# Memory keys and values of both layers from operands in two parts, the weights' second part made by a load that adds onto the negative of the first

## The chip, the cores and the metric

The program runs on one core of a Trainium2 chip. Its engines work side by side, each on its own list of instructions in order: TensorE (PE in the profile; its weight loads are PEld), VectorE (DVE), ScalarE (ACT), GpSimd (POOL) and SyncE (SP), which here only issues DMAs. An instruction starts when its engine has reached it and the semaphores that it waits for are there. The metric is the time of one execution on the device in microseconds (us), lower is better; the median of three runs is given with the lowest and the highest.

## The reference

One step of a streaming encoder of two layers, 1024 channels, 512 prompt tokens and 32 sample tokens. Layer 0 mixes tokens by an S5 state-space model with a gated output (GLU), layer 1 by retention. Each layer then attends to 256 memory tokens and ends in a ConvFFN. What the change touches are the memory's keys and values, which depend on the memory tokens and on weights alone:

```python
def memory_kv(mem, g_mem, w_kv):
    b, n, _ = mem.shape
    m = rms_norm(mem, g_mem).astype(F32) @ w_kv.astype(F32)
    k, v = jnp.split(m, 2, axis=-1)
    return k.reshape(b, n, MEM_HEADS, MEM_HD), v.reshape(b, n, MEM_HEADS, MEM_HD)
...
for i in range(DEPTH):
    ...
    xp = xp + yp                      # S5 or retention
    mkp, mvp = memory_kv(mem_prompt, norm_mem_kv[i], mem_w_kv[i])
    xp = xp + memory_attn(rms_norm(xp, norm_mem_q[i]), mkp, mvp, mem_w_q[i], mem_w_o[i])
```

What stands beside it in time is S5: a complex diagonal recurrence in 64 groups of 16 channels with 64 states each, `x[t] = a x[t-1] + b u[t]`, of which the output is the real part of `c x` and a direct term.

## The kernel before

**Products in two parts.** Most matrix products take each float32 operand as two float32r numbers, `hi` and `lo`, with `hi + lo` the operand, and add three products: hi·hi, hi·lo, lo·hi (`mm3`, L224 to L226). `weights` (L209) makes the parts of a weight tile of 128 x 1024: SyncE loads it into a buffer `wr` (L211), ScalarE copies it into `wh` as float32r (L206), and VectorE subtracts, `wl = wr - wh` (L207). There are three buffers each of `wr`, `wh` and `wl` in the whole program, used in turn.

**Phase 1** (`phase1`) holds S5 and, as fill for TensorE between S5's steps, the memory's projections of both layers. `kv_units` gives the latter as units: for each layer the operand (gain times memory, in eight pieces), then eight key tiles and eight value tiles, each with one weight tile of 512 KB. `KV_SPLIT` names the layers that work in two parts. Before it holds layer 1 alone. Layer 0's weights are just loaded, and one float32 product per piece is taken (L500); its operand is gain times memory by ScalarE. Layer 1's weights go through `weights`, its operand is made in two parts (ScalarE, then VectorE at L476), and its products are those of `mm3`. `product` (L495 to L500) chooses. The call `fill(us)` emits units until about so many microseconds of TensorE's work are used up, 3.5 for a tile: 0.5 at the start, 28 behind the discretisation, 2 and 13 around the norm of the inputs, and then what `PROLOGUE` and `ORDER` say.

**S5's steps** work on an eighth of the groups each, e = 0 to 7:

- `matrices(e)`: GpSimd scales the inputs, `u` (L781); VectorE multiplies powers of `a` with `b` (L789, L790), into buffers of the tags `wh` and `wl`, the same three each that the weights use; GpSimd adds (L791); TensorE turns the result (L797) and multiplies it with `c` (L802); ScalarE copies out (L798); GpSimd and VectorE make `Fg` (L807, L809), and eight DMAs lay it out.
- `states(e)`: TensorE multiplies with the inputs (L823); VectorE and GpSimd turn the result by phases (L834 and on for VectorE; L836, L839 and the copies L840, L841 for GpSimd); VectorE scans (L847, twice); both turn it back; GpSimd copies the states out (L859, L860).
- `carry(e)`: VectorE multiplies (L873 and on), GpSimd adds (L877). `outputs(e)`: TensorE multiplies (L888, L889), ScalarE applies gelu and copies.

The powers of phases that `states` needs are made once (`phases`; GpSimd's share stands at L553 and L556). The loop runs e from 0 to 7 in the order `S(e+1), C(e+1), O(e), F 4, M(e+2), F 5`, where F n is `fill(n)`; what is left of the units comes behind it. A scheduler then puts the instructions of the whole program into one order for each engine, by the dependences and the buffers; the order is fixed when the kernel is built.

**Behind phase 1** come GLU and everything else: `dense` products (L233) of the same form, with `weights` for each tile.

Of the kernel before, what the change touches and what calls it, by code (L numbers as in the profile page):

```python
# [9 lines left out]
F32 = mybir.dt.float32  # L10
# [7 lines left out]
P = 128  # L18
D = 1024
KT = D // P            # channel tiles  # L20
TP = 512               # prompt tokens
TS = 32                # sample tokens
# [3 lines left out]
NM = 256               # memory tokens  # L26
FF = 2816
NF = FF // P
H = 4                  # heads (memory attention and retention)
EPS = 1e-6  # L30
GN_EPS = 1e-5
G = 64                 # S5 groups
C = 16                 # channels of a group
NP = 32                # pairs of groups
L = 8                  # S5 chunk
POS = 70               # dummy, 64 prompt chunks, dummy, 4 sample chunks
SLOT = 560             # elements of a general slot
# phase 1: microseconds of TensorE's work on the memory's projections between the steps of S5
F_START, F_DISC, F_NORM, F_MAT = 0.5, 28, 2, 13
KV_US = 3.5  # L40
KV_SPLIT = (1,)          # layers whose memory projections take operands in two parts
KV_RMS, KV_ROW = 1, 4      # key tiles after which the memory's norm is worked out, and applied
# steps of S5 for an eighth of the groups (M matrices, P phases, S states, C carry, O outputs, F fill)
PROLOGUE = (("M", 0), ("P", 0), ("S", 0), ("M", 1), ("C", 0), ("F", 6))
ORDER = (("S", 1), ("C", 1), ("O", 0), ("F", 4), ("M", 2), ("F", 5))
FGROUPS = (8, 7, 7)    # ConvFFN tiles between down projections
# [6 lines left out]
def constants():  # L53
    """Arrays that depend on shapes alone."""
# [27 lines left out]
def w_tiles(w, mt=None):  # L82
    """[K, M] -> [m tile, 128 of k, K/128 * 128 of m]: one contiguous chunk for an output tile."""
    k, m = w.shape
    a = w.reshape(k // P, P, m // P, P).transpose(2, 1, 0, 3)
    return a.reshape(m // P, P, (k // P) * P)


def layout(inp):
# [10 lines left out]
    def cols(a):                      # [.., n*128] -> [128, .. * n]  # L100
        a = a.reshape(-1, a.shape[-1] // P, P)
        return a.transpose(2, 0, 1).reshape(P, -1)
# [3 lines left out]

    def pair(a):                      # [G, 64] -> [(g2, p), pair]
        return a.reshape(NP, P).T

    def both(a):                      # [G, 64] -> [(2, p), G]  # L110
        return np.concatenate([a.T, a.T], axis=0)
# [7 lines left out]
    cr, ci = f["ssm_c_re"][0], f["ssm_c_im"][0]      # [G, C, 64]  # L119
# [6 lines left out]
    rt, it = cr.transpose(2, 0, 1), ci.transpose(2, 0, 1)          # [64, G, C]  # L126
    ca = np.stack([np.concatenate([rt, it]), np.concatenate([it, rt])])   # [2, 128, G, C]
    d["ca"] = ca.reshape(2, P, KT, 8 * C).transpose(2, 1, 0, 3).reshape(KT, P, 256)

    def rows(a):                      # [1024] -> [(jj, c), G]  # L130
        return np.tile(a.reshape(G, C).T, (L, 1))

# [6 lines left out]
    # values: [layer, half of columns, quarter of k, 128, 2 k tiles * 512]  # L139
# [13 lines left out]
    d["w_r"] = w_tiles(wq)            # q 8, k 8, v 16, g 16 tiles  # L153
# [17 lines left out]
class Kernel:  # L171
# [7 lines left out]
    # ---- tiles  # L179
# [13 lines left out]
    def psum(self, name, two, one):  # L193
        """TensorE's accumulators of a part of the program: two banks each, and one each."""
        self.two, self.one = two, one
        return self.tc.tile_pool(name=name, bufs=1, space=PSUM)
# [7 lines left out]
    # ---- weights: loaded, and split into parts of 12 and 12 bits  # L204
# [15 lines left out]

    def mm3(self, out, a, b, start, stop):
        """out (+)= a^T b for operands in two parts."""
# [20 lines left out]
    def dense_open(self, src, xs):  # L243
        """The first operands of an output tile."""
        o = [self.ps(), self.weights(src), 0]
        self.dense_more(o, xs)
        return o
# [7 lines left out]
    def dense2(self, srcs, xs, late=1, hooks=()):  # L255
        """Two output tiles, the last operands of both behind all others; hooks go in between."""
# [15 lines left out]
    def parts(self, src):  # L272
        """src [P, T] -> its two parts, in general slots."""
# [4 lines left out]
    # ---- norms: operands are gain * x; 1 / rms comes in where a product leaves PSUM  # L278
# [29 lines left out]
    def rsqrt_of(self, m, r, tmp):  # L308
        """r = m^-1/2: a first guess from the exponent's bits, and three steps r <- r (1.5 - 0.5 m r^2)."""
# [13 lines left out]
    def resid_cols(self, ps):  # L323
        """1 / rms of the tokens, 128 of them in a column; ps [128, 5] of PSUM."""
# [12 lines left out]
    def along_row(self, ps, rc, blocks):  # L337
        """Columns rc laid along the free dimension of all partitions, in PSUM."""
# [3 lines left out]
    def resid_r(self):  # L342
        """Two hooks that give 1 / rms of the tokens along a row of all partitions, self.r."""
# [19 lines left out]
    # ---- program  # L363
# [28 lines left out]
    def final(self):  # L392
        """The last norm: turned to tokens by rows, scaled by 1 / rms where it leaves PSUM."""
# [30 lines left out]
    # ---- memory keys and values  # L424
    def kv_units(self):
        """The projections of both layers, in pieces that fill gaps: (microseconds of TensorE, emit)."""
# [22 lines left out]
        def rms():  # L449
            """1 / rms of the memory's tokens: along a row, and in columns."""  # L450
# [14 lines left out]
        def operand(l):  # L465
            """gain * memory"""
# [21 lines left out]
        def weights(l, src):  # L488
            if l in KV_SPLIT:
                return self.weights(src)  # L490
# [4 lines left out]
        def product(l, out, a, ca, b, cb, k):  # L495
            """out (+)= a[:, ca]^T b[:, cb], in one or in two parts."""
# [50 lines left out]
    # ---- S5  # L547
    def cmul(self, eng, o, a, b, t, eng2=None):
        """o = a b of complex pairs; t: two temporaries of the same shape. o may not alias a or b."""
# [9 lines left out]
    def phase1(self, sp):  # L559
# [43 lines left out]
        # inputs in the S5 layout: [(7 - token of chunk, channel), group, chunk]  # L603
# [4 lines left out]
        # discretisation, for columns of pairs (32) and of groups (64)  # L608
# [8 lines left out]
        def exp_acc(out, x, t):  # L617
            """exp to float32's accuracy: 2^k times a polynomial."""
# [33 lines left out]
        # powers 0..8 of a = rho (cos, sin)  # L652
# [18 lines left out]
        # b_bar = (a - 1) / lam * b, times the norm's gains  # L671
# [23 lines left out]
        # u = x / rms(x)  # L695
# [26 lines left out]
        # unit phases of a^8 to the power of the chunk, and its magnitude  # L722
# [7 lines left out]
        def unit(c):  # L730
            """c / |c|, for |c| near 1"""
# [43 lines left out]
        def matrices(e):  # L775
            """What a chunk's inputs give to the state at its end, and to its own outputs."""
# [5 lines left out]
            # a^lag b_bar, as [(g2, p), pair, lag, c]; the second holds minus the imaginary part  # L782
# [31 lines left out]
        def states(e):  # L814
            """Chunk inputs to the state, turned back by the chunk's phase, scanned, turned forth."""
# [46 lines left out]
        def carry(e):  # L862
            """What the state before a chunk gives to its tokens: Re(c a^(l+1) x)."""
# [72 lines left out]
    # ---- memory attention  # L936
    def attention(self, ap, l):
# [33 lines left out]
        def soft(rows, b0, b1, src, pr, st):  # L971
            """Softmax of scores / 16, whose queries still lack 1 / rms."""
# [30 lines left out]
        def turn(pr, pss):  # L1003
            """The weights, keys by rows."""
# [4 lines left out]
            # the sample's, from the cache  # L1009
# [53 lines left out]
    # ---- ConvFFN  # L1063
    def ffn(self, l):
# [11 lines left out]
        for n, size in enumerate(FGROUPS):  # L1076
            ys = []
            for _ in range(size):
# [3 lines left out]
                # [2 zeros, prompt, 2 cached rows, sample]  # L1082
# [26 lines left out]
    # ---- retention  # L1109
    def retention(self, rp):  # L1110
# [26 lines left out]
        def rope(tile0):  # L1137
            """Two tiles of a projection, rotated: in float32, and in parts."""
# [32 lines left out]
        def scores(d, h):  # L1171
            d.decay = decay = st([P, TP], "decay")
            nc.sync.dma_start(out=decay, in_=io["decay"][h])
            # keys by token, with the decay to the end
# [14 lines left out]
            # the sample's scores  # L1189
# [4 lines left out]
            # scores with decay, [key, query]  # L1194
# [34 lines left out]
        def outputs(d, h):  # L1229
            """By token, normalised."""  # L1230
# [48 lines left out]
        def gated(d, h):  # L1279
            """By feature."""  # L1280
# [61 lines left out]
def collect(o):  # L1342
    y = o["y"]
    ssm = o["ssm"].reshape(2, 64, 2, G).transpose(2, 0, 3, 1)         # [segment, re/im, G, 64]
# [17 lines left out]
```

## Time and profile before

| | |
|---|---|
| median of 3 runs | 1894.64 us (1894.32 to 1896.23) |
| span of the profiled execution, first to last instruction | 1893.0 us |
| mean granted TensorE clock | 0.980 |
| 0 to 247.86 us (up to the first product of GLU): PE, DVE, ACT, POOL busy | 192.63, 224.00, 74.28, 165.22 us |
| 247.86 to 1893.00 us: PE, DVE, ACT, POOL busy | 1627.52, 862.66, 537.28, 219.50 us |

Of the profiled execution only the span is given, and no time of its own beside it. How to read the profile: a row of a group names the line, the engine, the operation, output and inputs by the program's names, the shape and how often it came; then busy us, the mean of one in ns, and the idle time of the engine ahead of it with what ended it. A row of the timeline begins with the start in us, counted from the first instruction, and the length; in brackets stands what the engine waited for. Rows of stretches have the busy time of each engine, the granted clock and the DMA engines' share. A DMA row ends in the median of the time from issue to landing. Names are without buffer numbers: `wr`, `wh`, `wl` are those of above, `u` the inputs, `xl` the turned matrices, `r` and `xh` general slots.

### The profile page before, as it was taken

Reading aid. Unit: us, or ns where it says so; the run is one execution under the profiler, and the core shown is the slowest. Engines: PE = TensorE matmul, PEld = TensorE weight load, DVE = VectorE, ACT = ScalarE, POOL = GpSimd, SP = SyncE. Lnnn points to the kernel's source line nnn. Section 1 sums busy time; section 2 is a strip of 40 time slices with the busy share of each in tenths; the row PEclk is TensorE's granted clock in tenths of the full one; section 3 lists DMA queues with packets and bytes.
Section 4 is the critical chain, followed back from the end, with each engine's and each line's share of the span. In section 5 each row is a group of like instructions: output and inputs, shape, how many; then the busy total and the mean of one; then the engine's idle time right before and its main releaser. Section 6 shows DMA issues by size and latency. Waiting matters only on the chain.

```text
span 1893.0 us, 32752 instructions
## 1 busy us (share of the span) xinstructions
PE 1820.2 (96%) x13785; PEld 1730.6 (91%) x13785; DVE 1086.7 (57%) x1848; ACT 611.6 (32%) x901; POOL 384.7 (20%) x439
## 2 busy tenths in 40 slices
PE   7868899999999999999999999999999999999998
PEld 6457789999999999999899899998999999999998
DVE  9999856545544535555644646546655554453553
ACT  3132454433323323333223122223444332232333
POOL 7685611011211202121000100100101121120221
PEclk9888989999999999999999999999999999999998
DMA  6434344122222222232222222222411222222221
GB/s 214 132 114 124 120 133 144 68 86 79 90 90 88 78 92 90 72 109 82 76 85 94 79 79 73 90 79 86 138 68 56 87 84 88 90 84 95 90 71 67
DMA packets 65970, 178.02 MB, mean 94 GB/s; under 512 B 8928, under 2 KB 18528, under 8 KB 65824
## 3 DMA queue, kind: packets, MB, share of 16 engines
q1 hardware_dynamic: 65536, 175.79, 27.4%
q8 instruction: 108, 1.77, 0.4%
q14 instruction: 38, 0.31, 0.1%
q10 hardware_dynamic: 288, 0.15, 0.0%
HBM read 162.78 MB, written 10.77 MB: 92 GB/s over the span
## 4 chain that ended last, share of the span: by engine, by line
PE 83%; DVE 2%; issue 1%; ACT 1%; ACTq 0%; DVEq 0%
PE ps L233 74%; PE ps L224 2%; PE ps L225 2%; PE ps L226 2%; PE ps L1286 1%; DVE wl L207 0%; PE ps L1275 0%; PE ps L1248 0%; PE ps L1008 0%; PE ps L1222 0%; ACT wh L206 0%; PE bank L1022 0%; DVE xl L292 0%; PE ps L329 0%; PE ps L403 0%
## 5 line engine op out<-in xcount | busy, mean ns | idle before, releaser
L206 ACT CAST wh<-wr 128x1024 fp32r<-128x1024 f32 (+1 forms) x256 | 264.6, 1037 | 810.2 <-PE ps L233 626.8
L233 PE MATMUL ps<-xh,wh 128*128 128x272 f32 x2432 | 507.5, 290 | 5.4 <-DVE x L356 3.6
L233 PE MATMUL ps<-xl,wh 128*128 128x272 f32 x2432 | 503.6, 288 | 0.0
L233 PE MATMUL ps<-xh,wl 128*128 128x272 f32 x2432 | 502.3, 288 | 0.0
L233 PE MATMUL ps<-r,wh 128*128 128x272 f32 x2688 | 449.2, 289 | 3.0 <-ACT r L901 1.6
L233 PEld LDWEIGHTS ps<-xh,wh 128*128 128x128 f32 x2432 | 380.7, 188 | 11.1 <-ACT r L298 3.7
L233 PEld LDWEIGHTS ps<-r,wh 128*128 128x128 f32 x2688 | 380.2, 189 | 6.4 <-ACT r L206 3.0
L233 PEld LDWEIGHTS ps<-xh,wl 128*128 128x128 f32 x2432 | 382.0, 188 | 2.3 <-issue 2.3
L233 PEld LDWEIGHTS ps<-xl,wh 128*128 128x128 f32 x2432 | 383.0, 189 | 0.3
L207 DVE TENSOR_TENSOR wl<-wr,wh 128x1024 fp32r<-128x1024 f32 (+1 forms) x256 | 321.8, 1260 | 92.3 <-ACT wh L206 84.2
L233 PE MATMUL ps<-r,wl 128*128 128x272 f32 x1344 | 278.0, 288 | 0.0
L233 PEld LDWEIGHTS ps<-r,wl 128*128 128x128 f32 x1344 | 211.2, 189 | 0.0
L356 DVE TENSOR_TENSOR x<-ps,x 128x544 f32<-128x544 f32 x96 | 69.3, 724 | 234.9 <-PE ps L233 234.7
L301 POOL TENSOR_TENSOR acc<-acc,r 128x544 f32<-128x544 f32 x36 | 58.8, 1633 | 453.1 <-ACT r L298 444.6
L1088 POOL COPY nco<-r 128x2 f32<-128x2 f32 x44 | 13.9, 315 | 374.5 <-DVE r L1086 374.5
L1095 DVE TENSOR_TENSOR r<-ps,rr 128x544 f32<-128x544 f32 x44 | 31.9, 725 | 96.7 <-PE ps L233 96.7
L1085 DVE TENSOR_TENSOR r<-ps,rr 128x272 f32<-128x272 f32 x44 | 19.4, 442 | 117.4 <-PE ps L233 117.4
L1146 POOL TENSOR_TENSOR r<-r,r 128x544 f32<-128x544 f32 x8 | 10.8, 1353 | 339.9 <-ACT wh L206 326.0
L1096 POOL TENSOR_TENSOR r<-r,r 128x32 f32<-128x32 f32 x44 | 34.3, 780 | 206.2 <-ACT wh L206 186.2
L206 ACT CAST r<-r 128x544 fp32r<-128x544 f32 x84 | 52.5, 650 | 65.8 <-POOL r L1096 26.2
L1093 DVE SCALAR_TENSOR_TENSOR r<-r,conv,r 128x546 f32<-128x546 f32 x88 | 69.1, 785 | 3.5 <-ACT r L1091 1.9
L207 DVE TENSOR_TENSOR r<-r,r 128x544 fp32r<-128x544 f32 x84 | 59.3, 729 | 14.5 <-ACT r L206 14.3
(354 smaller groups left out, 2109.0 us busy)
## 6 DMA issues: line engine op xcount, KB each, us to landing
wr<-in_w_r SPq DMA_DIRECT2D x48, 512.0 KB, 3.2
wr<-in_w_a SPq DMA_DIRECT2D x44, 512.0 KB, 3.2
wr<-in_w_g SPq DMA_DIRECT2D x44, 512.0 KB, 3.2
wr<-in_w_d SPq DMA_DIRECT2D x32, 448.0 KB, 3.2
wr<-in_w_k SPq DMA_DIRECT2D x16, 512.0 KB, 4.9
wr<-in_w_v SPq DMA_DIRECT2D x16, 512.0 KB, 3.6
wr<-in_w_q SPq DMA_DIRECT2D x16, 512.0 KB, 4.0
wr<-in_w_o SPq DMA_DIRECT2D x16, 512.0 KB, 3.3
```

The source lines that it names most:

```text
L206: self.nc.scalar.copy(hi, src)
L207: (self.nc.gpsimd if pool else self.nc.vector).tensor_tensor(out=lo, in0=src, in1=hi.bitcast(F32), op=OP.subtract)
L224: mm(out, lhsT=a[0], rhs=b[0], start=start, stop=False)
L225: mm(out, lhsT=a[0], rhs=b[1], start=False, stop=False)
L226: mm(out, lhsT=a[1], rhs=b[0], start=False, stop=stop)
L233: mm(ps[:, h, :TH], lhsT=ws[wi], rhs=x[xi][:, h * TH:(h + 1) * TH], start=start and n == 0, stop=stop and n == 2)
L301: add.tensor_tensor(out=self.acc, in0=self.acc, in1=sq, op=OP.add)
L356: self.nc.vector.tensor_tensor(out=self.halves(x), in0=src, in1=self.halves(x), op=OP.add)
L1085: V.tensor_tensor(out=ext[:, 2:2 + TH], in0=pa[:, 0, :TH], in1=r[:, :TH], op=OP.mult)
L1093: V.scalar_tensor_tensor(out=cv, in0=ext[:, t:t + W], scalar=cw[:, t, f:f + 1], in1=cv, op0=OP.mult, op1=OP.add)
L1095: V.tensor_tensor(out=self.halves(gr), in0=pg[:, :, :TH], in1=self.halves(r), op=OP.mult)
L1096: PL.tensor_tensor(out=gr[:, TP:], in0=gr[:, TP:], in1=cv[:, TP + 2:W], op=OP.mult)
```

## The change

Both layers now work in two parts, and the weight tiles of the memory's projections no longer come through `weights` but through a new function. In it ScalarE makes the first part as before, then writes the negative of it to `lo`; and GpSimd issues a second load of the same tile from memory that adds onto what stands in `lo`. VectorE's subtraction falls away for these tiles. GLU and the rest keep `weights`. Comments and docstrings are gone from the code as well, and with the new function all lines behind L221 stand 11 further on (L834 is L845, L791 is L802).

```diff
-KV_SPLIT = (1,)          # layers whose memory projections take operands in two parts
+KV_SPLIT = (0, 1)
...
+    def weights_loaded(self, src):
+
+        raw = self.main.tile([P, 1024], F32, tag="wr", bufs=3, name=self.name("wr"))
+        self.nc.sync.dma_start(out=raw, in_=src)
+        hi = self.main.tile([P, 1024], F32R, tag="wh", bufs=3, name=self.name("wh"))
+        lo = self.main.tile([P, 1024], F32R, tag="wl", bufs=3, name=self.name("wl"))
+        self.nc.scalar.copy(hi, raw)
+        self.nc.scalar.activation(out=lo, in_=hi.bitcast(F32), func=AF.Copy, scale=-1.0)
+        self.nc.gpsimd.dma_start(out=lo, in_=src, accum_op=OP.add)
+        return hi, lo
...
         def weights(l, src):
             if l in KV_SPLIT:
-                return self.weights(src)
+                return self.weights_loaded(src)
```

What this does to the order on the engines is shown at three places. A row has the line, the operation, the output and its inputs with their buffer numbers, and the shape of the output. First GpSimd where the inputs of S5 are scaled (L781, now L792); L229 is the adding load, `in_w_k` and `in_w_v` the weights of keys and values. Before:

```order
L556 TENSOR_TENSOR r_703<-ph_518 128x512
L781 TENSOR_TENSOR u_158<-u_158,ur_463 128x560
...
L781 TENSOR_TENSOR u_165<-u_165,ur_463 128x560
L836 TENSOR_TENSOR r_742<-r_742,r_743 128x280
L839 TENSOR_TENSOR r_742<-r_742,r_743 128x280
L840 COPY r_742<-s_22_153 128x4
```

With the change:

```order
L567 TENSOR_TENSOR r_948<-ph_763 128x512
L229 DMA wl_506<-in_w_k 128x1024
L229 DMA wl_544<-in_w_v 128x1024
L229 DMA wl_671<-in_w_v 128x1024
L792 TENSOR_TENSOR u_191<-u_191,ur_656 128x560
...
L792 TENSOR_TENSOR u_198<-u_198,ur_656 128x560
L229 DMA wl_690<-in_w_v 128x1024
L229 DMA wl_709<-in_w_v 128x1024
L229 DMA wl_736<-in_w_v 128x1024
L802 TENSOR_TENSOR wh_773<-wh_773,wl_774 128x512 x2
```

Before the scaling stand ten adding loads in all, the last three of them shown, and behind it three more, those of the 11th to the 13th tile; then come the sums of the first matrices (L802, before L791), which before stood ahead of the scaling.

Second, TensorE at the first matrices of S5 (L797 and L802, now L808 and L813) and the first products of the states (L823, now L834); L500 is layer 0 before, L235 to L237 the three products now. Before:

```order
L500 MATMUL bank_500<-wr_501,r_102 128x512
L797 MATMUL bank_538<-ident,wh_528 128x128 x4
L797 MATMUL bank_544<-ident,wh_528 128x128 x4
L802 MATMUL bank_550<-wh_528,cbd_525 32x128 x8
L500 MATMUL bank_499<-wr_829,r_105 128x512
...
L500 MATMUL bank_500<-wr_835,r_108 128x512
L823 MATMUL bank_724<-u_158,xl_536 64x70 x5
```

With the change:

```order
L236 MATMUL bank_732<-wl_736,r_110 128x512
L237 MATMUL bank_732<-wh_735,r_110 128x512
L808 MATMUL bank_783<-ident,wh_773 128x128 x4
L808 MATMUL bank_789<-ident,wh_773 128x128 x4
L813 MATMUL bank_795<-wh_773,cbd_770 32x128 x8
L235 MATMUL bank_731<-wh_1076,r_113 128x512
L235 MATMUL bank_732<-wh_1076,r_113 128x512
L834 MATMUL bank_969<-u_191,xl_781 64x70 x8
```

The matrices now stand behind the 13th layer-0 tile, whose second part, `wl_736`, is the last of the three loads that GpSimd issues behind the scaling.

Third, GpSimd in one round of the loop, from a carry's sum (L877, now L888) to the copy of the states (L859, now L870). Before:

```order
L877 TENSOR_TENSOR xl_1112<-xl_1112,r_1113 128x512
L791 TENSOR_TENSOR wh_1433<-wh_1433,wl_1434 128x512 x2
L836 TENSOR_TENSOR r_1321<-r_1321,r_1322 128x280
L839 TENSOR_TENSOR r_1321<-r_1321,r_1322 128x280
L840 COPY r_1321<-s_22_153 128x4
...
L807 TENSOR_TENSOR Fg_1676<-gu_145,lag_19_147 128x128
L859 COPY stout_510<-r_1341 128x8
```

With the change:

```order
L888 TENSOR_TENSOR xl_1397<-xl_1397,r_1398 128x512
L229 DMA wl_1559<-in_w_k 128x1024
L229 DMA wl_1687<-in_w_k 128x1024
L802 TENSOR_TENSOR wh_1722<-wh_1722,wl_1723 128x512 x2
L847 TENSOR_TENSOR r_1609<-r_1609,r_1610 128x280
L850 TENSOR_TENSOR r_1609<-r_1609,r_1610 128x280
...
L818 TENSOR_TENSOR Fg_1967<-gu_178,lag_25_180 128x128
L229 DMA wl_1770<-in_w_k 128x1024
L870 COPY stout_755<-r_1629 128x8
```

The issues of the loads stand between GpSimd's own steps of S5, ahead of the sum of the matrices and behind the start of `Fg`.

## The prediction

> **What bounds the kernel now.** I read the page's summary first, then the chain of waits that ended last, then busy times by stretches. Columns of the second fence: start, us, what. In the third: stretch, its length, then busy us (instructions) of each engine, the granted clock, DMA's share, GB/s.
> ```profile
> span 1893.0 us, 32752 instructions
> PE 1820.2 (96%) x13785; PEld 1730.6 (91%) x13785; DVE 1086.7 (57%) x1848; ACT 611.6 (32%) x901; POOL 384.7 (20%) x439
> PE   7868899999999999999999999999999999999998
> DVE  9999856545544535555644646546655554453553
> ```
> ```profile
> 247.86 58.73 PE ps L233 x455
> ```
> ```profile
> 0.00:41.66 41.66, 33.04 (x150) 28.68 (x150) 37.86 (x134) 15.94 (x29) 27.66 (x30) 0.96 0.69 243
> 50.00:88.30 38.30, 31.40 (x116) 15.08 (x116) 36.28 (x100) 3.69 (x6) 23.71 (x24) 0.91 0.45 141
> 88.30:247.86 159.56, 123.40 (x1030) 104.64 (x1026) 141.52 (x193) 54.27 (x105) 105.61 (x109) 0.87 0.38 117
> sum 247.86, PE 192.63 PEld 152.15 DVE 224.00 ACT 74.28 POOL 165.22; mean PE 48.16 PEld 38.04 DVE 56.00 ACT 18.57 POOL 41.30
> ```
> From 247.86 us on TensorE is full with L233, and those 1645 us hold nothing that the change touches: behind phase 1 each engine's order is unchanged. Before 247.86 VectorE is the full one (224.0 of 247.86 us), with GpSimd passing work to and fro. So the change is worth what it does to the moment when phase 1 ends. The times of before come from one execution with a span of 1893.0 us; the median shown, 1894.64, lies 1.64 above it, and I add the sum to that median. About 0.2% (3.8 us) is what a measurement of this kernel can tell from no change.
>
> **The change, part by part.** *What it removes.* The subtractions that make the second part of layer 1's weights:
> ```profile
> L207 DVE TENSOR_TENSOR wl<-wr,wh 128x1024 fp32r<-128x1024 f32 x19 | 28.5, 1512 | 0.1
> L476 DVE SCALAR_TENSOR_TENSOR r<-r,gains,r 128x256 fp32r<-128x256 f32 x8 | 5.7, 773 | 0.0
> L790 DVE TENSOR_TENSOR wl<-PIn,bbi 128x512 f32<-128x512 f32 x3 | 2.0, 681 | 0.0
> L206 ACT CAST wh<-wr 128x1024 fp32r<-128x1024 f32 x19 | 20.0, 1051 | 51.4 <-PE bank L226 24.8 <-PE bank L225 18.8 <-DMA wr<-in_w_k 7.8
> ```
> Nineteen tiles, of which three are GLU's: 16 x 1.512 = 24.2 us less on VectorE, all inside S5's loop. *What it adds there:* layer 0's operand in two parts, 8 x 0.773 = 6.2 us. ScalarE gets 16 first parts and 32 negatives of 1.05 us, some 50 us beside 74.3 of 247.86, and it is idle most of the time: hidden, except that each negative stands 1.05 us ahead of its load. TensorE's layer-0 tiles change from float32 to three products:
> ```profile
> 90.20 5.42 PE L500 MATMUL bank<-wr,r 128*128 128x512 f32 x12
> 193.41 0.48 PE L224 MATMUL bank<-wh,r 128*128 128x512 f32 x1
> 196.24 0.40 PE L224 MATMUL bank<-wh,r 128*128 128x512 f32 x1
> ```
> A float32 tile is eight such instructions, 5.42 x 8 / 12 = 3.61 us; a tile in two parts is twelve, of which the 1st and 13th start 2.83 us apart. It saves 0.8 us a tile on an engine that isn't the bound here: nothing by itself.
>
> *The new chain.* Each of 32 tiles now goes load, ScalarE (first part), ScalarE (negative), GpSimd (issues the adding load), landing, TensorE. Before's trace shows neither an adding load nor an issue on GpSimd. Landing: between plain loads of the same size in the quiet part and the slowest tensor of phase 1,
> ```profile
> wr<-in_w_r SPq DMA_DIRECT2D x48, 512.0 KB, 3.2
> wr<-in_w_k SPq DMA_DIRECT2D x16, 512.0 KB, 4.9
> u<-in_U SPq DMA_DIRECT2D x8, 280.0 KB, 7.1
> ```
> so 3.2 to 7.1 us; I take 4.9, which the same tensor takes in this phase. (The Trainium skill, "DMA: Bandwidth & Descriptors", Anatomy of one DMA, gives 2.0 us + bytes / 436e3 for a load that GpSimd issues, by which 524288 bytes would take an estimated 3.2 us and the sum below would come out near its lower end; no run here shows an adding one.) Issue: SyncE needs 0.33 us for one; GpSimd's work on 128 partitions beside a busy VectorE goes up to 4.97.
> ```profile
> 84.05 0.33 SPq L211 DMA_DIRECT2D wr<-in_w_k  x1
> 45.09 4.97 POOL L556 TENSOR_TENSOR r<-ph 128x32 f32<-128x32 f32 x1
> 64.62 0.63 POOL L556 TENSOR_TENSOR r<-ph 128x224 f32<-128x224 f32 x1
> ```
> I take 1.0, nearer to the undisturbed 0.63 than to the disturbed 4.97. A transfer that costs less than nothing is excluded: the chain only gets links.
>
> *Where it is waited for, first place: the start of S5's loop.* Before, TensorE had turned the first S5 matrices (L797) between layer-0 tiles, and VectorE started the first state (L834) just behind the first scaled input:
> ```profile
> 85.61 12.24 POOL L781 TENSOR_TENSOR u<-u,ur 128x560 f32<-128x560 f32 x8 [4.19 <-DVE ur L315]
> 78.76 1.04 PE L797 MATMUL bank<-ident,wh 128*128 128x128 f32 x8
> 79.39 1.07 ACT L798 COPY xl<-bank 128x512 f32<-128x512 f32 x2 [3.18 <-PE bank L797]
> 86.94 0.58 PE L823 MATMUL bank<-u,xl 128*64 128x70 f32 x10 [1.21 <-POOL u L781]
> 88.30 0.43 DVE L834 TENSOR_TENSOR r<-bank,ph 128x280 f32<-128x280 f32 x1
> ```
> In the new order GpSimd scales all eight inputs and only then issues the loads of tiles 11, 12 and 13; TensorE has these three tiles ahead of its first S5 matrix. I leave the scaling at 85.61: VectorE has 6.2 us more ahead of it, but the twelve products L789/L790 (12 x 0.68 = 8.2 us) have moved behind it, since their buffers are now the weights'. GpSimd's own earlier issues fall into its waits for VectorE (4.19 here and more before). Then: scaling done 97.85, issue 98.85, landed 103.75, three tiles 8.5 (the next landings hide beside TensorE) 112.2, L797 to both copies 1.7 (78.76 to 80.46), L823 to the first L834 1.36: 115.3 instead of 88.30, **+27.0**. Queued behind the waiting TensorE are all S5 products; behind those wait ScalarE's copies and VectorE.
>
> *Second place: each round of the loop.* One round of before, VectorE and GpSimd:
> ```profile
> 167.68 0.43 DVE L834 TENSOR_TENSOR r<-bank,ph 128x280 f32<-128x280 f32 x1
> 168.39 2.29 DVE L207 TENSOR_TENSOR wl<-wr,wh 128x1024 fp32r<-128x1024 f32 x1
> 172.81 1.37 DVE L847 TENSOR_TENSOR_SCAN r<-d,r 128x280 f32<-128x280 f32 x2 [1.42 <-POOL r L840]
> 183.06 2.35 DVE L207 TENSOR_TENSOR wl<-wr,wh 128x1024 fp32r<-128x1024 f32 x2
> 188.28 0.43 DVE L834 TENSOR_TENSOR r<-bank,ph 128x280 f32<-128x280 f32 x1
> ...
> 166.70 2.90 POOL L791 TENSOR_TENSOR wh<-wh,wl 128x512 f32<-128x512 f32 x2 [3.57 <-DVE wh L789]
> 171.12 0.79 POOL L836 TENSOR_TENSOR r<-r,r 128x280 f32<-128x280 f32 x1 [1.52 <-DVE r L835]
> 171.87 0.77 POOL L839 TENSOR_TENSOR r<-r,r 128x280 f32<-128x280 f32 x1
> 176.50 0.60 POOL L807 TENSOR_TENSOR Fg<-gu,lag 128x128 f32<-128x128 f32 x1
> ```
> The 20.60 us hold three subtractions. The first (2.29) stands where VectorE would wait for GpSimd anyway: with an issue ahead of L791 the scan comes after 1.0 + 2.90 + 1.69 (L836 to the scan, 171.12 to 172.81) = 5.6 us instead of 5.13, so nothing is gained. The other two (2.35) lie in the 15.47 us behind the scan: VectorE alone would need 5.6 + 13.1 = 18.7. But another issue stands behind L807: 5.6 + 4.3 (172.81 to 177.1) + 1.0 + 4.9 until the tile lands, 2.83 for it on TensorE, then L823 to L834 1.36: **20.0**, later than VectorE, so 0.6 saved a round, 4.2 in the seven rounds to the last state. What is queued behind these issues on GpSimd are S5's own sums, for which VectorE's scan waits. By the bounds: with 3.2 to land and 0.33 to issue VectorE decides, 4.9 + 13.1 = 18.0, saving 2.6 x 7 = 18.2 against a start only 24.6 later, +6.4; with 7.1 a round takes 22.2, and 29.2 + 11.2 = +40.4.
>
> The stretch from the last state to GLU stays as it is. **Sum: 27.0 - 4.2 = +22.8 us: 1915.8 of span, 1917.4 against the median.**
>
> **Rivals.** *A smaller loss* (0.12): the loop runs at VectorE's pace, from +6.4 to +12.0 (a landing of 3.2 with an issue of 1.0: 25.3 - 1.9 x 7), about 1904. For it: VectorE's 95% before. *Cancelled* (0.08): all 24.2 come out of the loop, 27.0 - 24.2 = +2.8, 1897.4; against it speaks the wait at the scan. *Faster* (0.10): VectorE bounds phase 1 whatever the order, 224.0 - 24.2 + 6.2 = 206.0 with the same 23.9 idle, 229.9: -18.0, 1876.7. It decides if the thirteen layer-0 tiles are through TensorE by the time the inputs are scaled (98 us); the order speaks against it. *GpSimd choked* (0.08): each issue takes as long as L553's worst,
> ```profile
> 41.76 3.38 POOL L553 TENSOR_TENSOR r<-ph 128x32 f32<-128x32 f32 x1 [0.26 <-DVE mt L314]
> ...
> L553 POOL TENSOR_TENSOR r<-ph 128x480 f32<-128x480 f32 (+4 forms) x6 | 8.7, 1454 | 10.4 <-DVE ph L737 6.0 <-DVE ut L313 4.2 <-DVE mt L314 0.3
> ```
> 3.4 us where 0.63 was enough for seven times the elements. Ten issues ahead of the scaling cost 10 x 2.4 = 24, of which GpSimd's waits there (10.4 ahead of L553, 4.2 ahead of L781) take up 14.6, so 9.4; the three tiles behind it 2.4 + 2 x (3.4 - 2.83) = 3.5; two issues a round on the path 4.8 x 7 = 33.6: 22.8 + 46.5 = +69, 1964. The Trainium skill, "SBUF — State Buffer", Who interferes with whom, says that descriptors of a load issued by GpSimd wait while VectorE holds the shared ports in its two-port modes, and infers that two-input products do not hold them so: by that rule the choking would be rare in this loop. *That it doesn't do what it says* would need tiles that miss the new branch; both layers take it.
>
> **How the numbers follow.** Likeliest, 0.62: 1917.4, and by its bounds 1905 to 1935. Slower 0.62 + 0.12 + 0.08 = 0.82, same 0.08, faster 0.10. The range 1896 to 1938 takes in the loss of every landing between the bounds and the cancelled case, and leaves out the faster and the choked one, 0.18.
>
> **What would show it.** VectorE's first state (L834, then L845) near 115 us, with TensorE waiting for tiles 11 to 13 ahead of it; later starts of that line some 20 us apart; the end of phase 1 near 271; VectorE idle at the scan for GpSimd and at the first product of each round for TensorE. A first state before 100 us, or rounds of 17 us, would make it wrong.

## The result, and the profile after

| | before | with the change |
|---|---|---|
| median | 1894.48 us (1891.91 to 1896.23, 4 runs) | 1919.27 us (1910.41 to 1920.47, 4 runs) |
| profiled execution, span | 1893.0 us | 1908.4 us (that execution: 1910.41 us) |

The ratio is 1.0122, with a 95% interval of 1.0099 to 1.0145: slower by 24.8 us in the medians. The profiled execution is the fastest of its four, 15.4 us of span above before; a second profile, below, is of an execution of 1921.45 us, the slowest of its own four. First the page of the changed kernel: span, busy times, and the busy tenths of TensorE, VectorE and GpSimd in 40 slices of 47.7 us.

```profile
span 1908.4 us, 33072 instructions
PE 1809.0 (95%) x13881; PEld 1736.3 (91%) x13881; DVE 1064.6 (56%) x1840; ACT 658.5 (35%) x949; POOL 394.8 (21%) x471
PE   4668889999999999999999999999999999999998
DVE  8678766555544545556554555546655554454543
POOL 6667721011210201221010000100201121120221
```

VectorE's busy time went down by 22.1 us (1086.7 to 1064.6), and the time went up. Behind phase 1 nothing moved. In the stretches of both kernels (length, then busy us and instructions of PE, PEld, DVE, ACT and POOL, granted clock, DMA share, GB/s) the first ends with VectorE's first state, the second with its last one, the third with the first product of GLU. Before:

```profile
0.00:88.30 88.30, 69.23 (x277) 47.51 (x279) 82.48 (x253) 20.01 (x36) 59.61 (x55) 0.90 0.54 182
88.30:226.92 138.62, 109.51 (x953) 92.52 (x950) 128.63 (x175) 46.37 (x88) 96.97 (x99) 0.88 0.36 112
226.92:247.86 20.94, 13.89 (x80) 12.12 (x78) 12.89 (x19) 7.90 (x17) 8.64 (x10) 0.84 0.52 152
```

After:

```profile
0.00:108.59 108.59, 61.82 (x346) 55.34 (x348) 80.72 (x256) 46.40 (x62) 67.44 (x70) 0.75 0.76 206
108.59:239.41 130.82, 101.94 (x949) 87.38 (x944) 106.83 (x161) 63.94 (x107) 96.34 (x113) 0.93 0.74 187
239.41:263.08 23.67, 17.66 (x112) 15.04 (x110) 14.77 (x21) 11.02 (x21) 11.47 (x14) 0.93 0.78 196
263.08:1908.40 1645.32, 1627.59 (x12485) 1578.59 (x12485) 862.27 (x1405) 537.11 (x762) 219.59 (x276) 1.00 0.26 87
```

The first state comes 20.29 us later, the seven rounds to the last one are 7.80 shorter, the stretch to GLU is 2.73 longer: +15.2 in sum, and the 1645 us behind are the same. The start is the chain that the prediction followed. The next rows are from the timeline of the changed kernel, GpSimd, TensorE and VectorE (start, length, what; in brackets the idle time ahead and what ended it).

```profile
80.78 9.96 POOL L792 TENSOR_TENSOR u<-u,ur 128x560 f32<-128x560 f32 x8 [4.22 <-DVE ur L326]
90.69 2.62 POOL L229 DMA_DIRECT2D wl<-in_w_v  x3
102.40 3.38 POOL L802 TENSOR_TENSOR wh<-wh,wl 128x512 f32<-128x512 f32 x2 [9.09 <-DVE wh L800]
96.17 0.80 PE L236 MATMUL bank<-wl,r 128*128 128x512 f32 x1 [6.22 <-DMA wl<-in_w_v]
105.61 1.04 PE L808 MATMUL bank<-ident,wh 128*128 128x128 f32 x8
100.42 0.69 DVE L801 TENSOR_TENSOR wl<-PIn,bbi 128x512 f32<-128x512 f32 x1 [17.38 <-PE bank L236]
108.59 0.45 DVE L845 TENSOR_TENSOR r<-bank,ph 128x280 f32<-128x280 f32 x1 [1.05 <-PE bank L834]
```

All eight inputs are scaled at 90.7 us, the three loads are issued behind them, and TensorE stands idle for 6.22 us until the first has landed; three tiles later, at 105.61, it turns the first matrix. VectorE's products for that matrix were late as well: VectorE stood idle for 17.38 us until TensorE had used the weights that held their buffers, and GpSimd then waited 9.09 us for them at L802. Both paths end within about a microsecond of each other here.

In the loop VectorE has 21.8 us less to do (128.63 to 106.83) and 14.0 us more idle time (10.0 to 24.0); the difference is the 7.8 us. Its longest waits between the first and the last state (us in total, times, the longest), and then the longest one before:

```profile
DVE r L858 <- POOL r L851: 13.1, 6, 2.5
DVE wl L801 <- PE bank L236: 6.2, 2, 4.5
DVE wh L800 <- PE bank L236: 1.7, 1, 1.7
DVE r L845 <- PE bank L834: 1.1, 1, 1.1
```

```profile
DVE r L847 <- POOL r L840: 7.0, 5, 2.4
```

And the loads (median us from issue to landing), and TensorE's waits for them in phase 1:

```profile
wr<-in_w_k SPq DMA_DIRECT2D x16, 512.0 KB, 6.2
wl<-in_w_k POOLq DMA_DIRECT2D x16, 512.0 KB, 6.4
wr<-in_w_v SPq DMA_DIRECT2D x16, 512.0 KB, 4.4
wl<-in_w_v POOLq DMA_DIRECT2D x16, 512.0 KB, 8.3
```

```profile
PE bank L236 <- DMA wl<-in_w_v: 20.0, 5, 6.2
PE bank L237 <- DMA wl<-in_w_k: 18.9, 8, 7.2
```

So TensorE waited 38.9 us for adding loads, in 13 waits, 14.3 us of it in the loop and 3.8 in the stretch to GLU; before there was none of this kind.

### The profile page after: what moved, and what is told of

Same layout as the page of the kernel before. It is cut to its first block, busy times and chain, and to the rows that moved or that the text cites. A ratio compares the mean times of both kernels' runs of the same rounds, so it can differ in the third digit from the quotient of the medians.

```text
span 1908.4 us, 33072 instructions
## 1 busy us (share of the span) xinstructions
PE 1809.0 (95%) x13881; PEld 1736.3 (91%) x13881; DVE 1064.6 (56%) x1840; ACT 658.5 (35%) x949; POOL 394.8 (21%) x471
## 4 chain that ended last, share of the span: by engine, by line
PE 85%; DVE 6%; DMA 3%; issue 2%; POOL 2%; ACT 1%; SPq 0%; POOLq 0%; DVEq 0%; ACTq 0%
PE ps L244 74%; PE ps L235 2%; PE ps L236 2%; PE ps L237 2%; DMA wl<-in_w_v 1%; DMA wl<-in_w_k 1%; PE bank L236 1%; PE bank L237 1%; PE ps L1297 1%; PE bank L235 1%; POOL u L792 0%; DVE wl L207 0%; PE ps L1286 0%; DMA out_kT<-rr 0%; PE ps L1259 0%
## 5 line engine op out<-in xcount | busy, mean ns | idle before, releaser
L206 ACT CAST wh<-wr 128x1024 fp32r<-128x1024 f32 (+1 forms) x240 | 247.6, 1036 | 767.5 <-PE ps L244 640.9
L244 PEld LDWEIGHTS ps<-xh,wh 128*128 128x128 f32 x2432 | 380.8, 188 | 11.2 <-ACT r L309 3.8
L207 DVE TENSOR_TENSOR wl<-wr,wh 128x1024 fp32r<-128x1024 f32 (+1 forms) x240 | 297.7, 1243 | 94.4 <-ACT wh L206 85.6
L207 DVE TENSOR_TENSOR r<-r,r 128x544 fp32r<-128x544 f32 x84 | 59.3, 728 | 11.3 <-ACT r L206 11.2
```

The lines of the kernel that those rows point to most:

```text
L206: self.nc.scalar.copy(hi, src)
L207: (self.nc.gpsimd if pool else self.nc.vector).tensor_tensor(out=lo, in0=src, in1=hi.bitcast(F32), op=OP.subtract)
L244: mm(ps[:, h, :TH], lhsT=ws[wi], rhs=x[xi][:, h * TH:(h + 1) * TH], start=start and n == 0, stop=stop and n == 2)
```

## The experiments

The theory: the loss is the chain SyncE's load, ScalarE twice, GpSimd's issue, landing, TensorE's tile, which stands on the path ahead of the first state and in the rounds; without it, VectorE's missing subtractions would have made the kernel faster. The rivals: the second reading of the weights crowds the DMA engines; layer 0 in two parts costs by itself; GpSimd's issues cost by themselves. All kernels are the changed one with the edit shown. Two of them (no adding load, plain load by GpSimd) leave out a part of the computation, the right second part of the weights, and serve for the time alone. The table has the medians, the ratio to before on the same chip, and from each profile the first state, the seven rounds, the stretch from the last state to GLU, and the end of phase 1, all in us.

| | median | ratio (95%) | first state | rounds | to GLU | end |
|---|---|---|---|---|---|---|
| before | 1894.48 | | 88.30 | 138.62 | 20.94 | 247.86 |
| the change | 1919.27 | 1.0122 (1.0099 to 1.0145) | 108.59 | 130.82 | 23.67 | 263.08 |
| the change again | 1918.2 | 1.0130 (1.0115 to 1.0145) | 108.79 | 139.08 | 26.37 | 274.24 |
| layer 1 alone | 1901.93 | 1.0040 (1.0027 to 1.0054) | 88.39 | 140.57 | 25.66 | 254.62 |
| loads for layer 0 alone | 1916.69 | 1.0124 (1.0110 to 1.0138) | 107.91 | 140.69 | 19.65 | 268.25 |
| no adding load | 1881.34 | 0.9935 (0.9921 to 0.9948) | 95.52 | 119.73 | 18.15 | 233.40 |
| three tiles fewer at the start | 1912.7 | 1.0101 (1.0087 to 1.0114) | 99.65 | 132.62 | 37.05 | 269.32 |
| subtractions, both layers | 1917.8 | 1.0127 (1.0114 to 1.0141) | 124.11 | 127.89 | 19.32 | 271.32 |
| negative first | 1910.98 | 1.0087 (1.0073 to 1.0101) | 104.68 | 136.83 | 19.64 | 261.15 |
| plain load by GpSimd | 1895.52 | 1.0010 (1.0001 to 1.0019) | 103.49 | 127.08 | 19.42 | 249.99 |
| no split | 1886.57 | 0.9963 (0.9949 to 0.9976) | 101.89 | 119.84 | 17.93 | 239.66 |
| no split, other order | 1894.63 | 1.0003 (0.9994 to 1.0012) | 93.22 | 137.93 | 19.81 | 250.96 |

**Layer 1 alone.**

```diff
-KV_SPLIT = (0, 1)
+KV_SPLIT = (1,)
```

> Layer 0 goes back to one float32 product and plain loads; only layer 1's second parts come by the adding load. Theory (the loss sits ahead of the first state, where GpSimd issues layer 0's loads behind the scaling of the inputs; the loop gains from VectorE's missing subtractions): first state near 88 us as in before, the last four rounds 17.5 us each instead of 19.4, the stretch behind the last state 2.7 us longer, sum -5: 1885 to 1895 us. Rival (the second reading of the weights crowds the DMA engines and every load of phase 1 comes late): half of the traffic stays, so about +8: 1900 to 1905 us. Rival (layer 0 in two parts costs its own work on VectorE and TensorE): same forecast as the theory, told apart by the runs without the adding load and with fewer tiles ahead of the first state.

A miss: 1901.93 us, which lies within what the rival of traffic had forecast (1900 to 1905). The first state is back at 88.39, so the start's loss belongs to layer 0's tiles; but the rounds are 140.57 us, no shorter than before, though the 24 us of subtractions are gone from VectorE. One round alone, the fourth, lasts 33.2 us. In it TensorE, then VectorE (a state's first product, and the two long waits ahead of the next):

```profile
146.66 0.58 PE L237 MATMUL bank<-r,wl 128*128 128x256 f32 x1 [5.61 <-DMA wl<-in_w_k]
168.75 0.58 PE L237 MATMUL bank<-r,wl 128*128 128x256 f32 x1 [5.76 <-DMA wl<-in_w_k]
141.67 0.44 DVE L845 TENSOR_TENSOR r<-bank,ph 128x280 f32<-128x280 f32 x1
150.00 0.29 DVE L820 TENSOR_TENSOR Fg<-bank,Fg 128x128 f32<-128x128 f32 x1 [6.82 <-PE bank L816]
173.72 0.42 DVE L532 TENSOR_TENSOR acc<-bank,mr 128x256 f32<-128x256 f32 x1 [4.67 <-PE bank L237]
174.88 0.45 DVE L845 TENSOR_TENSOR r<-bank,ph 128x280 f32<-128x280 f32 x1
```

TensorE waits twice for an adding load, and each time VectorE then waits for TensorE, at `Fg` (L820) and at the copy of the keys (L532). I had taken the rounds of 17.5 us from the first profile of the change for layer 1's own pace; in this profile they are not. In this loop the loads took back all that the subtractions gave. Whether the second reading makes them late, or the chain alone, this run doesn't say.

**Loads for layer 0 alone.**

```diff
-                return self.weights_loaded(src)
+                return self.weights_loaded(src) if l == 0 else self.weights(src)
```

> Layer 0 as in the change (two parts, adding load); layer 1's second parts by VectorE's subtraction as in before. Theory: the loss at the start stays whole (first state near 108 us, 20 later than before), the rounds of layer 1 are as long as before (19 to 20 us): +18 to +25, 1910 to 1920 us. Rival (traffic): half of it, about +8 to +12: 1902 to 1907 us. Rival (layer 0 in two parts by itself): as the theory.

As the theory had it: first state at 107.91, the rounds at 140.69 us, 1916.69 us. The rival of traffic had forecast 1902 to 1907 us with half of the second reading gone. (The half that is gone belongs to the rounds, so this run says nothing of traffic at the start.)

**No adding load.**

```diff
-        self.nc.gpsimd.dma_start(out=lo, in_=src, accum_op=OP.add)
```

> The adding load is left out, so that the second part is only the negative of the first (part of the computation is missing); all else stands: two parts in both layers, ScalarE's two passes, VectorE without subtractions. Theory: TensorE's thirteen layer-0 tiles wait for no load behind the scaling, so the first state comes at 85 to 95 us, rounds at VectorE's pace of 17 to 18 us: 1878 to 1892 us, faster than before. Rival (layer 0 in two parts costs by itself): still +8 or more, over 1902 us. Rival (traffic): fast as well, since the traffic is gone.

1881.34 us, 13 less than before and 37 to 38 less than the change. The rounds take 17.1 us each. The stretches of this run:

```profile
0.00:95.52 95.52, 68.28 (x445) 59.78 (x446) 89.48 (x260) 53.60 (x74) 62.29 (x56) 0.84 0.55 183
95.52:215.25 119.73, 91.08 (x862) 79.62 (x859) 103.00 (x157) 58.53 (x97) 88.42 (x98) 0.90 0.39 123
```

The gain is real, then, and two parts in layer 0 by themselves are not what makes the change slow: they cost 7.2 us at the start, where VectorE is now busy 89.48 of 95.52 us, the loop gives 18.9, and the stretch to GLU 2.8. The adding loads, with all that comes with them, are the loss. This run takes away GpSimd's issues, the traffic and the wait at once; the next three take these apart, though not all the way.

**Three tiles fewer at the start.**

```diff
-F_START, F_DISC, F_NORM, F_MAT = 0.5, 28, 2, 13
+F_START, F_DISC, F_NORM, F_MAT = 0.5, 28, 2, 2
```

> The fill ahead of S5's matrices is 2 instead of 13, so that three layer-0 tiles fewer stand ahead of the first state and no adding load stands between the scaling and the first matrices; loads and work are the same in number. Theory: first state near 96 us (scaling to 91, GpSimd's sums of the matrices 3, TensorE 2), rounds 18 to 19 us, the last one no longer short of tiles (+5): 1906 to 1914 us, some 8 less than the change. Rivals (traffic, or the two parts of layer 0 by themselves): the first state stays at 105 us or later, and the time is 1917 us or more.

The same loads, issues and bytes, yet the first state comes at 99.65 instead of 108.59. Up to 80 us the traffic is the same (a DMA share of 0.78 against 0.77), and the scaling begins at 80.31 instead of 80.78: what waited there was the order. (From 80 to 99.65 us the share is 0.30 against 0.90, since the loads now stand behind; that a fuller queue makes a landing longer this run doesn't exclude.) The three tiles come back at the end, where the stretch to GLU grows from 23.67 to 37.05. Phase 1 of this profile ends at 269.32, between the two profiles of the change; the median is 6.6 below the change's, and by the ratios, each to before on its own chip, the gain is 4 to 5.5 us.

**Negative first.** ScalarE writes the negative from the loaded tile, and the first part behind it.

```diff
-        self.nc.scalar.copy(hi, raw)
-        self.nc.scalar.activation(out=lo, in_=hi.bitcast(F32), func=AF.Copy, scale=-1.0)
+        self.nc.scalar.activation(out=lo, in_=raw, func=AF.Copy, scale=-1.0)
         self.nc.gpsimd.dma_start(out=lo, in_=src, accum_op=OP.add)
+        self.nc.scalar.copy(hi, raw)
```

> ScalarE writes the negative first, straight from the loaded tile, and the first part behind it, so that each adding load can be issued one pass (1.05 us) earlier; the work is the same. Theory (load, ScalarE, GpSimd, landing, TensorE is one chain on the path): 1 us less on each tile that TensorE waits for, and one tile fewer behind the scaling; first state 103 to 107 us, in all 4 to 12 us less than the change: 1907 to 1915 us. Rival (GpSimd's issues or the traffic are the cost, not the length of the chain): within 3 us of the change.

1910.98 us, 7 to 8 less than the change, for two lines in another order: the same issues, the same bytes, the same passes. Only the chain is shorter, by one pass of ScalarE. (In the new order two adding loads instead of three stand behind the scaling, too; the two effects come together here. The first state comes 4 us earlier, and the stretch to GLU is 4 to 7 us shorter.)

**Plain load by GpSimd.**

```diff
-        self.nc.scalar.activation(out=lo, in_=hi.bitcast(F32), func=AF.Copy, scale=-1.0)
-        self.nc.gpsimd.dma_start(out=lo, in_=src, accum_op=OP.add)
+        self.nc.gpsimd.dma_start(out=lo, in_=src)
```

> GpSimd's load brings the tile itself into the second part, without adding, and ScalarE's negative is left out (part of the computation is missing: the second part is the whole weight). GpSimd's 32 issues and the second reading of the weights stay; the load no longer stands behind SyncE's load and ScalarE's two passes. Theory (what costs is the length of the chain load, ScalarE twice, issue, landing): 2.1 us and more off each tile that TensorE waits for, twice what the negative first gave: first state 96 to 104 us, 1890 to 1906 us. Rival (GpSimd's issues and the traffic cost by themselves): no better than with the negative first, 1908 us or more. The landing time beside the adding load's 6.4 and 8.3 us is the price of adding.

1895.52 us. GpSimd's loads of this run, as on its page, and then TensorE's wait for the loads of the values' second parts, with 0.5 us more for those of the keys:

```profile
wl<-in_w_k POOLq DMA_DIRECT2D x16, 512.0 KB, 5.3
wl<-in_w_v POOLq DMA_DIRECT2D x16, 512.0 KB, 4.2
```

```profile
PE bank L235 <- DMA wl<-in_w_v: 9.0, 5, 3.9
```

Some 23 us of the loss go with the chain and with the adding, which this run takes away together. A load that adds took a median of 7.4 us over all 32 in the change, a plain one by the same engine, for the same bytes, 4.9. Beside the run without the adding load 14.2 us are left (1895.52 - 1881.34): 32 issues on GpSimd (0.53 to 0.72 us each, where the adding ones take 0.84 to 1.58), the second reading, and another order. These were not told apart further, and that stays open. The other loads landed late beside the adding loads, and hardly beside plain second ones: SyncE's loads of the keys' weights took 6.2 us to land beside the adding loads, and those of the inputs 11.8; beside as many plain ones 5.2 and 8.2, with no second load 5.1 and 7.4. So a part of the 23 us may be crowding, too.

**Subtractions, both layers.**

```diff
-                return self.weights_loaded(src)
+                return self.weights(src)
```

> Both layers in two parts, all second parts by VectorE's subtraction, no adding load. Theory: VectorE has 13 x 1.5 us of subtractions and 6.2 us of operands more ahead of the first state, 26 us, which it has no room for: first state near 114 us, then rounds as in before (19 to 20 us): 1917 to 1928 us, not better than the change. Rival (GpSimd's queue and the loads are all of the loss): without them the first state comes at 95 us or earlier, 1895 to 1905 us.

1917.8 us, no better than the change (1918.2 on the same chip), by another way: the first state at 124.11 (expected near 114), with VectorE busy 118.01 of those 124.11 us, and then shorter rounds. Beside the loads for layer 0 alone, where layer 1 has subtractions as well (ratio 1.0124 against 1.0127), making layer 0's second parts costs the same by either way: one has no room on VectorE, the other stands in GpSimd's order.

**The change again.**

> The change once more, unchanged, for a second profile, since the first profiled execution (1910.41 us) lies 8 us below the other three. Theory: first state near 108 us again, and the difference lies in the rounds of the loop, where TensorE waits for adding loads that take 5 to 11 us to land; median 1912 to 1921 us. Rival (the clock that TensorE is granted): the rounds are as long as in the first profile, and what is longer stands behind phase 1.

The first state is where it was, 108.79, and phase 1 ends 11.2 us later. The rounds differ from the third on. The first profile of the change, from there:

```profile
149.56:188.05 38.49, 32.81 (x329) 29.80 (x330) 30.97 (x53) 18.19 (x30) 27.76 (x33) 1.00 0.75 181
188.05:239.41 51.36, 45.09 (x420) 38.47 (x416) 39.30 (x61) 26.86 (x45) 37.84 (x46) 0.97 0.72 185
```

The second:

```profile
150.19:194.96 44.77, 38.30 (x331) 35.07 (x333) 29.59 (x52) 18.33 (x30) 26.82 (x33) 0.87 0.66 156
194.96:247.87 52.91, 46.03 (x415) 38.92 (x412) 37.01 (x61) 26.23 (x45) 36.60 (x45) 0.94 0.72 174
```

Neither theory had this whole. Of the 11.2 us 8.3 lie in the rounds and 2.7 in the stretch to GLU, none behind it; but TensorE's waits for loads in the loop are nearly the same (15.9 us against 14.3), and 6.3 of the 8.3 us lie in two rounds in which the granted clock was 0.87 instead of 1.00, and TensorE busy 38.30 us instead of 32.81 for the same products. Why the clock was lower there the profile doesn't show.

**No split.** Both layers as layer 0 was before: one float32 product, plain loads by SyncE.

```diff
-KV_SPLIT = (0, 1)
+KV_SPLIT = ()
```

> Neither layer in two parts: both layers as layer 0 was in before (one float32 product, plain loads by SyncE), so that neither subtractions nor adding loads are left. Theory (what the loop gains when VectorE's subtractions go is real, 17 us a round in the run without the adding load, and only the loads take it back): first state at 88 us as in before, rounds 17 to 18 us, TensorE 0.8 us a tile longer and with room for it: 1876 to 1886 us, faster than before. Rival (TensorE becomes the bound, with 3.6 us for each of layer 1's tiles): rounds of 19 us or more, 1890 to 1897 us.

1886.57 us, faster than both kernels (0.9963, 0.9949 to 0.9976). The rounds are 17.1 us, as in the run without the adding load. The first state is 13.6 us late, which I hadn't expected. GpSimd and VectorE there:

```profile
89.19 1.11 POOL L567 TENSOR_TENSOR r<-ph 128x512 f32<-128x512 f32 x1
90.26 4.96 POOL L792 TENSOR_TENSOR u<-u,ur 128x560 f32<-128x560 f32 x4
91.50 1.33 DVE L568 TENSOR_TENSOR ph<-ph,wt 128x32 f32<-128x32 f32 x1
92.73 1.33 DVE L743 TENSOR_TENSOR wt<-ph 128x32 f32<-128x32 f32 x1
93.99 1.30 DVE L744 TENSOR_TENSOR wt<-ph 128x32 f32<-128x32 f32 x1
95.33 0.19 DVE L745 TENSOR_TENSOR wt<-wt,wt 128x32 f32<-128x32 f32 x1
```

Products of VectorE on 32 elements a partition take 1.3 us while GpSimd scales the inputs, each from about where one of GpSimd's begins to where the next one does, and 0.19 when it has done so. Eight of them stand there, from 86.18 to 95.29 us, some 8 us longer than at 0.2 each. The scheduler had put half of the scaling ahead of the phases' last products; before, all but two of these (L737) were done when the scaling began.

**No split, other order.**

```diff
-F_START, F_DISC, F_NORM, F_MAT = 0.5, 28, 2, 13
-KV_US = 3.5
-KV_SPLIT = (0, 1)
+F_START, F_DISC, F_NORM, F_MAT = 0.5, 35, 2, 2
+KV_US = 3.0
+KV_SPLIT = ()
...
-ORDER = (("S", 1), ("C", 1), ("O", 0), ("F", 4), ("M", 2), ("F", 5))
+ORDER = (("S", 1), ("C", 1), ("O", 0), ("F", 3.5), ("M", 2), ("F", 4.3))
```

> As the run without any split, with numbers of the fill under which the phases' last products stand ahead of the scaling of the inputs again on GpSimd, as in before. There the first state came 13.6 us later than in before, with nine small products of VectorE at 1.07 to 1.33 us each beside GpSimd's products, which take 0.2 us elsewhere. Theory (the two engines slow each other down, and the order decides what stands beside what): first state at 88 to 94 us, rounds of 17 us, 1872 to 1880 us. Rival (the first state is late for want of TensorE, which has the same tiles ahead of it): 100 us again, 1884 to 1888 us.

The first state came at 93.22, as the theory had it; the time did not: 1894.63 us, no difference from before. The first round is 26.4 us long. The scaling now stands in one piece ahead of everything else on GpSimd:

```profile
90.76 12.96 POOL L792 TENSOR_TENSOR u<-u,ur 128x560 f32<-128x560 f32 x8 [6.13 <-DVE ur L326]
103.68 2.92 POOL L802 TENSOR_TENSOR wh<-wh,wl 128x512 f32<-128x512 f32 x2
106.57 0.77 POOL L847 TENSOR_TENSOR r<-r,r 128x280 f32<-128x280 f32 x1
```

An earlier first product was worth little here, since the same state's sums (L847) wait behind the scaling: the first state came 8.7 us earlier than in the run without split, and the first round took 8.9 longer. The other six rounds are longer by 9.2 us together; the fill's numbers put more of TensorE's work between them (857 instructions in the seven rounds against 789), but what cost there was not traced. The first state is a good mark only as long as what stands behind it on GpSimd is the same.

## Why the prediction was right, and where its sizes were off

*The place and the sign.* All of the difference lies in phase 1, as forecast (the 1645 us behind it are equal to 0.2 us). The start loses, the loop gives part of it back, by the chain named. The runs without the load (37 us below the change), with the order changed (first state 9 earlier), with the chain one pass shorter (7 below) and with a plain load (23 below) show it, the last three each together with something else, as said there.

*The start, forecast +27.0, measured +20.3 and +20.5.* The term that is off is "I leave the scaling at 85.61": it began at 80.78 and took 9.96 us instead of 12.24, so it was done 7.1 us earlier. From there on the terms hold: issue and landing 5.5 (forecast 5.9), three tiles 9.4 (8.5), L808 to the first state 3.0 (3.1). I put 6.2 us of operands more ahead of it on VectorE and 8.2 of products behind it, and gave the difference no credit; the operands took 3.8 us, at 0.48 each instead of 0.77. That GpSimd's eight products were shorter goes with VectorE standing still beside them: in the four profiles in which VectorE had at most 0.42 us of work meanwhile they took 9.94 to 9.96 us, in six in which it worked for 10.5 us or more of them 11.71 to 13.06 (12.96 with no split and the other order), and in one in which that work was mostly products of 32 and 224 elements a partition 10.39. The rule that bears on it: the Trainium skill, "SBUF — State Buffer", Who interferes with whom, states that a VectorE instruction with two inputs in SBUF contends with one of GpSimd that reads SBUF. The prediction used only the part on the descriptors of GpSimd's loads. The trace agrees with the other: 1.3 us instead of 0.19 for small two-input products beside GpSimd, in the run without split.

*The rounds, forecast -4.2, measured -7.8 and +0.5.* 20.0 us a round against 18.7 and 19.9. Two sizes were off against each other. The landing that I took, 4.9 us, was too short (6.4 and 8.3). By the Trainium skill, "DMA: Bandwidth & Descriptors", Anatomy of one DMA, a load of GpSimd's takes 2.0 us + bytes / 436e3, an estimated 3.2 us; here even its plain loads took 4.2 and 5.3, and the measurement decides. And the scan comes 3.7 to 4.1 us behind the state in the last four rounds, not 5.6: I added the issue and all of L791 up from the state's first product, but the row of L791 that the prediction shows begins 0.98 us ahead of it, behind 3.57 us of idle time that takes up an issue. The step that failed in its form is where the tile delays VectorE: I had it at the first product of each state. There it waited 1.1 us once, so one of the signs named did not appear. It was late at the products for the matrices (L800, L801: 7.9 us), whose buffers TensorE's tile still held, and in the second profile at the copies of the keys, too. The wait for GpSimd at the scan is there as forecast, 13.1 us in all, where before had 7.0.

*The stretch to GLU, forecast unchanged, measured +2.7 and +5.4.* Its last tiles are loaded by GpSimd as well, and TensorE waited 3.8 us for one; this was overlooked.

The sum of +22.8 lies between the two profiles, +15.4 and +26.4 of span, and near the +24.8 of the medians; this closeness is in part luck, since its errors partly cancelled (a start 7 too large, an end 3 to 5 too small, rounds off by 3.6 and 4.7, to either side). The 1905 of the likeliest case comes out of none of its sums, which give 1901.0 (+6.4) and 1906.6 (+12.0).

*The rivals.* GpSimd was not choked: its issues took 0.84 to 1.58 us, never 3.4. "Faster" is what the kernel does without the load, 1881 us, near the 1876.7 of that rival; the load stood in its way, as the order had shown. "Cancelled" supposed that all 24.2 us come out of the loop; even where nothing waits for a load only 18.9 do. The smaller loss wanted the loop at VectorE's pace (the 95% named for it are those of 50 to 88.30 us; in the rounds it was 92.8%), and its time, about 1904, lies below every run of the change.

## What to carry to other kernels

Work taken off the fullest engine is a gain only if the way round it isn't longer than the buffers allow to run ahead: here each tile's second part went through four links and a landing of 7 us with three buffers, and TensorE, for whose products VectorE and GpSimd waited, stood still for 38.9 us. Before a load is put on an engine that also computes, look at what stands ahead of it in that engine's order, and which tile of the consumer waits behind it. And ask first whether the work is needed: dropping the split altogether gave the same rounds of 17.1 us as leaving out the adding load did.

## What was not expected of the hardware

- A load that adds takes longer to land than a plain one by the same engine, for the same 512 KB: median 7.4 us over all 32 (5.3 to 11.2) against 4.9 (3.5 to 10.7), in two kernels that read the same bytes. It also holds GpSimd longer, 0.84 to 1.58 us an issue against 0.53 to 0.72, and the DMA engines: up to the first state they were busy for 0.76 of the time at 206 GB/s, with the plain loads for 0.65 at 222.
- Small two-input products on VectorE can run in step with GpSimd's: 1.07 to 1.33 us beside them, 0.2 alone, eight of eight in the run without split. Not always: in the changed kernel three of four took 0.20 us beside GpSimd's L714 (from 40.90 us), and the fourth 1.41. Larger ones slow each other down too: VectorE's products for the matrices took 1.75 us beside the scaling with three tiles fewer at the start, 0.69 behind it in the change, and the scaling 12.62 us instead of 9.96.
- The same rounds of the same kernel ran with TensorE's granted clock at 1.00 in one execution and at 0.87 in another, 38.5 us against 44.8.
